# Average pooling on one core: a tapered end with the last rows in seven shrinking pieces, and smaller transfers around it

## Chip, cores, metric

One core of a Trainium2 chip. The metric is the device time of one execution in microseconds (us). "Span" is the profiled execution from its first to its last instruction; the device time of the same execution is 1.7 to 2.0 us longer. Verdicts use a threshold of 2%.

## The reference

```python
x = randn(32, 256, 4096).astype(float32)      # output_size = 256
for i in range(256):
    result[:, :, i] = np.mean(x[:, :, 16*i : 16*(i+1)], axis=-1)
```

That is 8192 rows of 4096 numbers, each reduced to 256 means of 16 neighbours: 134.22 MB are read, 8.39 MB are written, and each number takes part in one addition.

## The kernel before

A tile is 256 rows: 128 partitions with two adjacent rows each, so a partition's share is one run of 32 KB in memory. The load is issued from SyncE's queue, VectorE reduces, ScalarE scales, and the store is issued from ScalarE's queue. Four input buffers and eight output buffers let the stages overlap.

```python
    RPP = 2
    tile_rows = P * RPP
    assert N % tile_rows == 0
    ntiles = N // tile_rows

    x_t = x_flat.rearrange("(n p r) l -> n p (r l)", p=P, r=RPP)
    o_t = out_flat.rearrange("(n p r) g -> n p (r g)", p=P, r=RPP)

    inv_w = 1.0 / float(window)

    in_pool = ctx.enter_context(tc.tile_pool(name="in_pool", bufs=4))
    out_pool = ctx.enter_context(tc.tile_pool(name="out_pool", bufs=8))

    for i in range(ntiles):
        xt = in_pool.tile([P, RPP * L], x.dtype)
        nc.sync.dma_start(out=xt, in_=x_t[i])

        sums = out_pool.tile([P, RPP * O], mybir.dt.float32)
        nc.vector.reduce_sum(
            out=sums,
            in_=xt.rearrange("p (g w) -> p g w", w=window),
            axis=mybir.AxisListType.X,
        )
        means = out_pool.tile([P, RPP * O], mybir.dt.float32)
        nc.scalar.mul(out=means, in_=sums, mul=inv_w)
        nc.scalar.dma_start(out=o_t[i], in_=means)
```

## Time and profile before

| | value |
|---|---|
| device time, median of 4 | 346.53 us |
| span | 344.7 us |
| VectorE busy | 277.9 us, 81% |
| DMA, loads and stores, share of 16 engines | 90.4% + 6.3% |
| last load landed (start of the last reduction) | 332.46 us |

Lines of the page of the kernel before. The two rows of digits cut the span into 40 slices, each digit the busy tenths of a slice (9 is 90% or more). The two queue lines give packets, MB and the share of all 16 DMA engines' time. The group lines give operation, shapes and count, then busy us and mean ns of one, then the idle time ahead of them and what ended it.

```profile
span 344.7 us, 255 instructions
DVE  0488898888898888898888898887898888898885
DMA  8999999999999999999999999999999999999950
q1 hardware_dynamic: 4608, 134.22, 90.4%
q10 hardware_dynamic: 4608, 8.39, 6.3%
L50 DVE TENSOR_REDUCE sums<-xt 128x512 f32<-128x8192 f32 x32 | 277.9, 8686 | 63.2 <-DMA xt<-in_x_dram 63.2
```

DMA is full in every slice between the ends, while VectorE, though 81% busy, waits before each reduction, and always for a load. So the DMA engines bound the kernel, except after the last load. The timeline of its end (start, duration, what; in brackets the idle time before):

```profile
332.46 8.69 DVE L50 TENSOR_REDUCE sums<-xt 128x512 f32<-128x8192 f32 x1 [1.63 <-DMA xt<-in_x_dram]
341.18 0.63 ACT L56 ACTIVATE means<-sums 128x512 f32<-128x512 f32 x1 [9.68 <-DVE sums L50]
341.84 0.34 ACTq L57 DMA_DIRECT2D out_dram<-means  x1
```

These run in series after the last load, 12.2 us of the span, and the DMA engines are nearly idle meanwhile (a share of 0.07 from 333 to 334 us, 0.00 from there to 341, and 0.15 to 0.19 for the last store).

### The profile page before, as it was taken

What the parts mean: (1) busy time and instruction counts of PE and PEld (TensorE: products, weight loads), DVE (VectorE), ACT (ScalarE), POOL (GpSimd) and SP (SyncE); (2) the same over time, 40 slices, a digit from 0 to 9 for tenths busy, and PEclk for the clock granted to TensorE, in tenths of its full rate; (3) what the DMA queues carried; (4) which work ended last, traced back from release to release, by engine and by line L of the source; (5) the groups of instructions that cost most, each with busy time, mean ns of one, the idle gap of its engine ahead of it and who ended that gap; (6) DMA issues with size and microseconds to landing.
All of it is one profiled execution on the core that took longest, in us unless ns stands there. A gap on an engine that the chain in (4) does not pass through costs nothing.

```text
span 344.7 us, 255 instructions
## 1 busy us (share of the span) xinstructions
DVE 277.9 (81%) x32; ACT 21.4 (6%) x33; POOL 0.2 (0%) x4
## 2 busy tenths in 40 slices
DVE  0488898888898888898888898887898888898885
ACT  1000000000000000000000000000000000000000
POOL 0000000000000000000000000000000000000000
DMA  8999999999999999999999999999999999999950
GB/s 335 437 430 407 452 433 413 443 437 412 448 441 417 431 445 409 443 445 432 412 453 421 423 449 432 408 454 428 416 449 429 412 453 432 412 449 432 408 239 30
DMA packets 9217, 142.62 MB, mean 414 GB/s; under 512 B 1024, under 2 KB 1024, under 8 KB 5120
## 3 DMA queue, kind: packets, MB, share of 16 engines
q1 hardware_dynamic: 4608, 134.22, 90.4%
q10 hardware_dynamic: 4608, 8.39, 6.3%
q14 instruction: 1, 0.01, 0.0%
HBM read 134.22 MB, written 8.39 MB: 414 GB/s over the span
## 4 chain that ended last, share of the span: by engine, by line
DMA 78%; DVE 20%; SPq 0%; issue 0%; ACT 0%; DVEq 0%
DMA xt<-in_x_dram 78%; DVE sums L50 20%; SPq L47 0%; ACT means L56 0%; DVEq L50 0%
## 5 line engine op out<-in xcount | busy, mean ns | idle before, releaser
L50 DVE TENSOR_REDUCE sums<-xt 128x512 f32<-128x8192 f32 x32 | 277.9, 8686 | 63.2 <-DMA xt<-in_x_dram 63.2
L56 ACT ACTIVATE means<-sums 128x512 f32<-128x512 f32 x32 | 20.1, 629 | 319.7 <-DVE sums L50 319.7
L56 ACT ACT_TABLE_LOAD x1 | 1.3, 1283 | 0.7 <-PEq L74 0.7
L74 POOL MEMSET const-uint8-127<- 128x1 uint8 x1 | 0.1, 103 | 0.0
L74 POOL MEMSET const-bfloat16-1.0<- 128x1 bf16 x1 | 0.1, 102 | 0.0
L74 POOL MEMSET const-float32-1.0<- 128x1 f32 x1 | 0.1, 100 | 0.0
L74 POOL MEMSET const-float32-0.0<- 128x1 f32 x1 | 0.1, 99 | 0.2 <-issue 0.2
## 6 DMA issues: line engine op xcount, KB each, us to landing
xt<-in_x_dram SPq DMA_DIRECT2D x32, 4096.0 KB, 32.5
out_dram<-means ACTq DMA_DIRECT2D x32, 256.0 KB, 15.0
```

The lines of the kernel that those rows point to most:

```text
L50: nc.vector.reduce_sum(out=sums, in_=xt.rearrange("p (g w) -> p g w", w=window), axis=mybir.AxisListType.X,)
L56: nc.scalar.mul(out=means, in_=sums, mul=inv_w)
L74: nc = _bacc.Bacc("TRN2", target_bir_lowering=False, num_devices=1)
```

## The change

Its intent is to make that end short. The last group of 128 rows is loaded and reduced in seven pieces of 928 down to 224 columns, so that little is left to reduce when the last one lands. Before it come 15 half-size groups (one row per partition) and three groups in two or three pieces. The scaling is in place, three large buffers replace four, and the first tile is half-size. Below, "the split" is the cutting of the last group into seven pieces, and "the taper" the shrinking groups before it. The core of the diff (`...` marks what is left out; comments in it are shortened or added):

```diff
-    RPP = 2
-    tile_rows = P * RPP
 ...
-    ntiles = N // tile_rows
+    TAIL_SPLITS = [[L]] * 12 + [
+        [L],
+        [L],
+        [L],
+        [2560, 1536],
+        [2304, 1792],
+        [1664, 1408, 1024],
+        [928, 800, 704, 608, 496, 336, 224],
+    ]
+    n_tail = len(TAIL_SPLITS)
+    n_main = (n_groups - 1 - n_tail) // RPP          # 22 large tiles
 ...
+    NIN = 3                                          # large buffers
+    NTFRESH = 5                                      # half-size buffers
 ...  (first group: 128 rows on its own, then n_main large tiles as before, scaled in place)
+    for j in range(n_tail):
+        splits = TAIL_SPLITS[j]
+        buf = tail_in[j]      # halves of the large buffers, the last five fresh
+        ssum = tail_sums[j][:, :]
+        last = j == n_tail - 1
+        c0 = 0
+        for k, cc in enumerate(splits):
+            c1 = c0 + cc
+            nc.sync.dma_start(out=buf[:, c0:c1], in_=x_flat[r0 : r0 + P, c0:c1])
+            nc.vector.reduce_sum(out=ssum[:, c0 // window : c1 // window], ...)
+            if last and k == len(splits) - 4:        # scale and store the first 190 means
+                ...
+            c0 = c1
+        # scale and store the rest of the group (the last 66 means of the last group)
```

More of the change, by code (lines that the diff above doesn't have):

```diff
@@ L30 @@
     N = x_flat.shape[0]
-    RPP = 2
-    tile_rows = P * RPP
-    assert N % tile_rows == 0
-    ntiles = N // tile_rows
-    x_t = x_flat.rearrange("(n p r) l -> n p (r l)", p=P, r=RPP)
-    o_t = out_flat.rearrange("(n p r) g -> n p (r g)", p=P, r=RPP)
-    inv_w = 1.0 / float(window)
-    in_pool = ctx.enter_context(tc.tile_pool(name="in_pool", bufs=4))
-    out_pool = ctx.enter_context(tc.tile_pool(name="out_pool", bufs=8))
-    for i in range(ntiles):
-        xt = in_pool.tile([P, RPP * L], x.dtype)
-        nc.sync.dma_start(out=xt, in_=x_t[i])
-        sums = out_pool.tile([P, RPP * O], mybir.dt.float32)
+    inv_w = 1.0 / float(window)
@@ new lines @@
+    fp32 = mybir.dt.float32
+    if N % P != 0 or L % window != 0:
+        ntiles = (N + P - 1) // P
+        xb = nc.alloc_sbuf_tensor("xb", [P, L], x.dtype)
+        sb = nc.alloc_sbuf_tensor("sb", [P, O], fp32)
+        for i in range(ntiles):
+            r0 = i * P
+            r1 = min(N, r0 + P)
+            rr = r1 - r0
+            nc.sync.dma_start(out=xb[0:rr], in_=x_flat[r0:r1])
+            nc.vector.reduce_sum(
+                out=sb[0:rr],
+                in_=xb[0:rr].rearrange("p (g w) -> p g w", w=window),
+                axis=mybir.AxisListType.X,
+            )
+            nc.scalar.mul(out=sb[0:rr], in_=sb[0:rr], mul=inv_w)
+            nc.scalar.dma_start(out=out_flat[r0:r1], in_=sb[0:rr])
+        return
@@ new lines @@
+    n_groups = N // P
+    RPP = 2
+    first_rows = 16
+    TAIL_SPLITS = [[L]] * 12 + [
[8 more added lines that the diff above has]
+    n_tail = len(TAIL_SPLITS)
+    for s in TAIL_SPLITS:
+        assert sum(s) == L
+    n_main = (n_groups - 1 - n_tail) // RPP
+    main_rows = n_main * RPP * P
+    assert n_main > 0
+    assert P + main_rows + n_tail * P == N, (P, main_rows, n_tail * P, N)
@@ new lines @@
+    r_main0 = P
+    x_main = x_flat[r_main0 : r_main0 + main_rows].rearrange(
+        "(n p r) l -> n p (r l)", p=P, r=RPP
+    )
+    o_main = out_flat[r_main0 : r_main0 + main_rows].rearrange(
+        "(n p r) g -> n p (r g)", p=P, r=RPP
+    )
+    r_tail0 = r_main0 + main_rows
+    NIN = 3
+    in_bufs = [
+        nc.alloc_sbuf_tensor(f"xin{i}", [P, RPP * L], x.dtype) for i in range(NIN)
+    ]
+    NTFRESH = 5
+    tail_bufs = [
+        nc.alloc_sbuf_tensor(f"xtail{i}", [P, L], x.dtype) for i in range(NTFRESH)
+    ]
@@ new lines @@
+    g0_buf = tail_bufs[0]
+    NSUM = 4
+    sum_bufs = [
+        nc.alloc_sbuf_tensor(f"sums{i}", [P, RPP * O], fp32) for i in range(NSUM)
+    ]
+    g0_sum = nc.alloc_sbuf_tensor("sumg0", [P, O], fp32)
+    tail_sums = [
+        nc.alloc_sbuf_tensor(f"sumt{i}", [P, O], fp32) for i in range(n_tail)
+    ]
+    nc.sync.dma_start(out=g0_buf[:, :], in_=x_flat[0:P, :])
+    nc.vector.reduce_sum(
+        out=g0_sum[:, :],
+        in_=g0_buf[:, :].rearrange("p (g w) -> p g w", w=window),
+        axis=mybir.AxisListType.X,
+    )
@@ L50 @@
+    nc.scalar.mul(out=g0_sum[:, :], in_=g0_sum[:, :], mul=inv_w)
+    nc.scalar.dma_start(out=out_flat[0:P, :], in_=g0_sum[:, :])
+    for i in range(n_main):
+        xt = in_bufs[i % NIN][:, :]
+        nc.sync.dma_start(out=xt, in_=x_main[i])
+        st = sum_bufs[i % NSUM][:, :]
         nc.vector.reduce_sum(
-            out=sums,
+            out=st,
             in_=xt.rearrange("p (g w) -> p g w", w=window),
@@ L54 @@
         )
-        means = out_pool.tile([P, RPP * O], mybir.dt.float32)
-        nc.scalar.mul(out=means, in_=sums, mul=inv_w)
-        nc.scalar.dma_start(out=o_t[i], in_=means)
+        nc.scalar.mul(out=st, in_=st, mul=inv_w)
+        nc.scalar.dma_start(out=o_main[i], in_=st)
+    reuse_order = [(n_main - 3 + k) % NIN for k in range(NIN)]
+    tail_in = []
+    for j in range(n_tail):
+        if j < n_tail - NTFRESH:
+            h = (j % 2) * L
+            tail_in.append(in_bufs[reuse_order[j // 2 % NIN]][:, h : h + L])
+        else:
+            tail_in.append(tail_bufs[j - (n_tail - NTFRESH)][:, 0:L])
+    for j in range(n_tail):
+        r0 = r_tail0 + j * P
+        splits = TAIL_SPLITS[j]
[6 more added lines that the diff above has]
+            nc.sync.dma_start(out=buf[:, c0:c1], in_=x_flat[r0 : r0 + P, c0:c1])
+            nc.vector.reduce_sum(
+                out=ssum[:, c0 // window : c1 // window],
+                in_=buf[:, c0:c1].rearrange("p (g w) -> p g w", w=window),
+                axis=mybir.AxisListType.X,
+            )
+            if last and k == len(splits) - 4:
+                g1 = c1 // window
+                nc.scalar.mul(out=ssum[:, 0:g1], in_=ssum[:, 0:g1], mul=inv_w)
+                nc.scalar.dma_start(
+                    out=out_flat[r0 : r0 + P, 0:g1], in_=ssum[:, 0:g1]
+                )
+            c0 = c1
+        if last:
+            g0c = (L - sum(splits[-3:])) // window
+            nc.scalar.mul(out=ssum[:, g0c:O], in_=ssum[:, g0c:O], mul=inv_w)
+            nc.scalar.dma_start(
+                out=out_flat[r0 : r0 + P, g0c:O], in_=ssum[:, g0c:O]
+            )
+        else:
+            nc.scalar.mul(out=ssum, in_=ssum, mul=inv_w)
+            nc.scalar.dma_start(out=out_flat[r0 : r0 + P, :], in_=ssum)
 _INS = ['x', 'output_size']
```

## The prediction

> **What bounds the kernel now.** The 16 DMA engines. The page's slices show DMA at 9 (90% or more) from slice 2 to slice 38, at about 430 GB/s, while VectorE is 81% busy (277.9 us) and every one of its idle gaps (63.2 us) ends on a load. The timeline shows a reduction every 10.32 us: 8.69 us of work and 1.64 us of waiting. So in steady state only DMA work counts. The exposed parts are the ends: data starts to flow at about 2 us, and after the last load lands (332.4 us) the timeline runs in series: last reduction 332.46 to 341.15 (8.69), scaling 0.63, store and end 2.9, to 344.7. This 12.3 us tail is all that a better schedule can win; the measured time is 1.85 us over the span.
>
> **What the change does.**
> 1. Tail: the last row group is loaded and reduced in 7 shrinking pieces, so the last reduction is 224 elements, not 8192. This is the gain.
> 2. Everything else makes more, smaller transfers: 52 loads instead of 32, 43 stores instead of 32; half-size tiles for 15 of the last groups and the first one. In-place scaling, three large buffers rather than four and the early small first tile touch nothing that bounds: a released buffer still has over 11 us of queued loads before it.
>
> **Costs.** From the page's DMA queue table I work out 1217 ns per 32 KB load packet and 85 ns per 2 KB store packet (share x span x 16 / packets that carry data). A line through both gives about 8.7 ns fixed per packet. [...] Per engine the loads grow from 256 to 416 data packets (+1.4 us) and stores from 256 to 344 (+0.8 us), semaphore packets add 0.3: +2.5 us in all, estimated, on engines that are saturated, so all on the critical path. The last load then lands at about 335.0, not 332.4.
>
> The VectorE tail: [...] A piece's load takes about 1.18 ns per element plus 0.08 us[...]. Then scaling of 66 columns 0.26, store and end 2.6.
>
> End of span: 335.0 + 2.0 + 0.3 + 2.6 = 339.9; plus 1.85 gives 341.7 us, 1.4% faster. Of 8.3 us of reduction taken out of the tail, 2.5 go to packets and 2.0 to the backlog. Range 339.3 to 343.6. Chances: faster by over 2% (under 339.6) 0.15, within 2% 0.83, slower 0.02.
>
> **What the profile would show.** Load packets 16 KB at about 611 ns and data packets per queue as counted; DMA still at 9 up to about 335; last reduction ending 1 to 2.7 us after the last landing, with the last pieces back to back; then under 3.2 us to the end; steady state 10.3 us per large tile.
>
> **What would make it wrong.** The fixed packet cost hidden by overlap (2 us faster); piece loads held back because DMA semaphores are shared by few loads and stores, or bubbles between small loads (1 to 3 us slower); a smaller fixed cost per reduction (1 us faster); reductions and loads of one buffer serialised by the dependency tracking (several us slower).

The sum came to 339.9 us of span and 341.7 us of time. The derivation of its term 2.0, the time from the last landing to VectorE's end (1.0 to 2.7), followed the pieces of the last three groups with a formula for the time of a reduction by its size, and the trace of the kernel before has one size alone (8192 elements, 8686 ns). So the 2.0 stands as estimate, not as something shown. The 8.7 ns come from the page's queue table. The trace of the changed kernel shows the time of a piece's load (its packets take 3.08 us per engine for 2560 elements and 1.01 for 800; the prediction's figures give 3.10 and 1.02) and the scaling of 66 columns (0.26 us); the store and end of 2.6 is an estimate from the 2.9 of the kernel before.

## The result

The changed kernel takes 340.39 us (340.28 to 340.55, 8 runs) against 346.53 us (346.40 to 346.64, 12 runs). The ratio is 0.9824, 95% interval 0.9814 to 0.9833: 1.8% faster, within 2%. (A ratio is the mean time of one kernel's runs over that of the other's of the same rounds, so not quite the ratio of the medians.)

The same lines of the page after, with the groups that take the place of L50:

```profile
span 338.8 us, 325 instructions
DVE  0588887988888988889888889887999988988996
DMA  8999999999999999999999999999999999999995
q1 hardware_dynamic: 7488, 134.22, 92.5%
q10 hardware_dynamic: 6192, 8.39, 6.7%
L114 DVE TENSOR_REDUCE sums<-xin 128x512 f32<-128x8192 f32 x22 | 191.1, 8686 | 39.6 <-DMA xin<-in_x_dram 39.6
L141 DVE TENSOR_REDUCE sumt<-xin 128x256 f32<-128x4096 f32 x14 | 61.6, 4416 | 7.6 <-DMA xin<-in_x_dram 7.6
L141 DVE TENSOR_REDUCE sumt<-xtail 128x256 f32<-128x4096 f32 (+14 forms) x15 | 22.6, 1568 | 0.9 <-DMA xtail<-in_x_dram 0.8
```

The empty last DMA slices are gone, and over the last groups VectorE waits only 0.9 us before 15 reductions. There are more packets for the same bytes. The end in the view of the chain that ended last (start, duration, what each next step waited for):

```profile
326.93 5.37 DMA out_dram<-sumt
332.30 0.02 issue
332.32 0.33 SPq L140
332.64 0.04 issue
332.69 2.96 DMA xtail<-in_x_dram
335.65 0.02 issue
335.67 0.40 DVE sumt L141
336.07 0.02 issue
336.09 0.26 ACT sumt L155
```

The last piece landed at 335.65, its reduction took 0.40 us, and 2.69 us after that the span ended. So the stretch after the last load shrank from 12.2 to 3.1 us, while the last load landed 3.2 us later (335.65 against 332.46); the difference is the 5.9 us by which the span is shorter. One step surprises: the loads of the last two pieces (SPq L140) were issued only when an earlier store had landed (DMA out_dram<-sumt, 5.37 us). The waits in the trace's semaphore records say why. All 95 DMAs of this trace, loads and stores alike, take turns on eight semaphores, and one that takes a semaphore waits here until the DMA before it on that semaphore has landed. The 336-column load got the semaphore of the store of the third-last group: that store landed at 332.30, the load was issued at 332.32, and the 224-column load stood behind it in the queue (332.69).

The sum of the prediction against the trace:

| term | predicted | measured |
|---|---|---|
| last load lands | 335.0 | 335.65 |
| VectorE ends after it | 2.0 | 0.42 |
| scaling, store, end | 2.9 | 2.69 |
| span | 339.9 | 338.76 |
| median device time minus this span | 1.85 | 1.63 |

### The profile page after: what moved, and what is told of

It is laid out like the page before. It is cut to its first block, busy times and chain, and to the rows that moved or that the text cites. A ratio compares the mean times of both kernels' runs of the same rounds, so it can differ in the third digit from the quotient of the medians.

```text
span 338.8 us, 325 instructions
## 1 busy us (share of the span) xinstructions
DVE 279.6 (83%) x52; ACT 23.7 (7%) x44; POOL 0.2 (0%) x4
## 4 chain that ended last, share of the span: by engine, by line
DMA 76%; DVE 22%; SPq 0%; issue 0%; ACT 0%; DVEq 0%
DMA xin<-in_x_dram 68%; DVE sums L114 18%; DMA xtail<-in_x_dram 7%; DVE sumt L141 4%; DMA out_dram<-sumt 2%; SPq L112 0%; ACT sumt L160 0%; SPq L140 0%; SPq L101 0%; ACT sumt L155 0%; DVEq L114 0%
## 5 line engine op out<-in xcount | busy, mean ns | idle before, releaser
L114 DVE TENSOR_REDUCE sums<-xin 128x512 f32<-128x8192 f32 x22 | 191.1, 8686 | 39.6 <-DMA xin<-in_x_dram 39.6
L141 DVE TENSOR_REDUCE sumt<-xin 128x256 f32<-128x4096 f32 x14 | 61.6, 4416 | 7.6 <-DMA xin<-in_x_dram 7.6
L119 ACT ACTIVATE sums<-sums 128x512 f32<-128x512 f32 x22 | 13.8, 629 | 217.0 <-DVE sums L114 217.0
L141 DVE TENSOR_REDUCE sumt<-xtail 128x256 f32<-128x4096 f32 (+14 forms) x15 | 22.6, 1568 | 0.9 <-DMA xtail<-in_x_dram 0.8
L160 ACT ACTIVATE sumt<-sumt 128x256 f32<-128x256 f32 x18 | 7.5, 416 | 79.9 <-DVE sumt L141 79.9
L102 DVE TENSOR_REDUCE sumg<-xtail 128x256 f32<-128x4096 f32 x1 | 4.4, 4420 | 8.3 <-DMA xtail<-in_x_dram 8.3
## 6 DMA issues: line engine op xcount, KB each, us to landing
xin<-in_x_dram SPq DMA_DIRECT2D x22, 4096.0 KB, 22.2
```

Of the source, the lines that this page charges most:

```text
L102: nc.vector.reduce_sum(out=g0_sum[:, :], in_=g0_buf[:, :].rearrange("p (g w) -> p g w", w=window), axis=mybir.AxisListType.X,)
L114: nc.vector.reduce_sum(out=st, in_=xt.rearrange("p (g w) -> p g w", w=window), axis=mybir.AxisListType.X,)
L119: nc.scalar.mul(out=st, in_=st, mul=inv_w)
L141: nc.vector.reduce_sum(out=ssum[:, c0 // window : c1 // window], in_=buf[:, c0:c1].rearrange("p (g w) -> p g w", w=window), axis=mybir.Axi ...
L160: nc.scalar.mul(out=ssum, in_=ssum, mul=inv_w)
```

## The experiments

Two theories of why 12 us of tail became only 6 us of gain. A, the prediction's: each packet has a fixed cost on saturated DMA engines, and a backlog on VectorE eats a part. B, the rivals: packets are free, and the gain went to held-back loads, to too few buffers, or to groups that do no good.

### Shorter runs in the kernel before

```diff
-    x_t = x_flat.rearrange("(n p r) l -> n p (r l)", p=P, r=RPP)
-    o_t = out_flat.rearrange("(n p r) g -> n p (r g)", p=P, r=RPP)
+    x_t = x_flat.rearrange("(n r p) l -> n p r l", p=P, r=RPP)
+    o_t = out_flat.rearrange("(n r p) g -> n p r g", p=P, r=RPP)
 ...  (the two DMAs view their tiles to match)
```

> The kernel before, with the two rows of a partition taken 128 rows apart instead of adjacent. Same DMA count, same bytes, same buffers, same reductions; only each contiguous run halves, 16 KB loads and 1 KB stores. Theory A (a fixed cost of about 8.7 ns per data packet on saturated DMA engines): per engine 256 more load packets and 256 more store packets, 512 x 8.7 ns = 4.5 us, so about 351.0 us (350.2 to 351.8). Theory B (the packet cost is hidden by overlap, and the change lost its gain to VectorE or to waits of the loads): unchanged, 346.5 within 0.5.

Measured: 348.88 us against 346.50, ratio 1.0069 (1.0054 to 1.0084). Both numbers missed. 512 more packets per engine cost 2.4 us, 4.6 ns each and not 8.7. In the packet records the durations still are 611 ns for 16 KB and 46 ns for 1 KB, as the line through two points said, and they sum to 4.2 us more per engine than before. But durations of packets overlap (in the steady phase they add up to 1.01 of the engines' time, as shown below), so their sum is more than the time.

### The taper taken out

```diff
 (lines joined here)
-    TAIL_SPLITS = [[L]] * 12 + [ [L], [L], [L], [2560, 1536], [2304, 1792], [1664, 1408, 1024],
-        [928, 800, 704, 608, 496, 336, 224] ]
+    TAIL_SPLITS = [ [928, 800, 704, 608, 496, 336, 224] ]
 ...
-    NTFRESH = 5
+    NTFRESH = 1
```

> The changed kernel without the tapering groups: large tiles up to the last group, and only that one in the seven pieces. Theory A (VectorE works off its last large tile only 11 to 16% faster than data arrives, so a backlog needs several small groups to vanish): the seven pieces land about 333, but VectorE starts them only after the last 8.7 us reduction and ends near 340.5, span 343, time 344.9 (344 to 346.2). Theory B (the small last piece alone wins the tail): about 338 to 339.5, faster than the changed kernel since it has fewer packets.

Measured: 345.42 us, ratio 0.997: theory A, 0.5 us above its number. The timeline of the end:

```profile
327.71 8.69 DVE L108 TENSOR_REDUCE sums<-xin 128x512 f32<-128x8192 f32 x1 [1.68 <-DMA xin<-in_x_dram]
328.24 0.88 SPq L134 DMA_DIRECT2D xtail<-in_x_dram  x2
336.31 4.76 DVE L135 TENSOR_REDUCE sumt<-xtail 128x58 f32<-128x928 f32 x7
```

The seven pieces wait behind the last large reduction and run back to back, with no gap, until 341.07; the last of their loads had landed at 333.8. Splitting the last group without the groups that grow smaller towards it wins 1.1 us of the 6.1.

### The last group whole, the taper kept

```diff
-        [928, 800, 704, 608, 496, 336, 224],
+        [L],
 (the early store of the last group's first means is dropped with it)
```

> The changed kernel with its last group of 4096 elements loaded and reduced whole, its taper kept. Theory A: the last load lands about 0.5 us sooner (48 packets fewer), then a full reduction of 4.42 us, scaling 0.42 and the store: about 343.9 us (343.2 to 344.6), 3.5 us slower than the changed kernel. Theory B (the last split is worth little, since packets and held-back issues take back what it gains): within 1 us of the changed kernel's 340.4.

Measured: 344.02 us, ratio 0.9928 (0.9911 to 0.9944): theory A to 0.1 us. The end of its timeline:

```profile
334.84 4.42 DVE L141 TENSOR_REDUCE sumt<-xtail 128x256 f32<-128x4096 f32 x1 [3.68 <-DMA xtail<-in_x_dram]
339.30 0.42 ACT L155 ACTIVATE sumt<-sumt 128x256 f32<-128x256 f32 x1 [7.69 <-DVE sumt L141]
```

So each alone gives much less than both: the taper alone wins 2.5 us, the split alone 1.1, together 6.1.

### Three buffers

```diff
-    in_pool = ctx.enter_context(tc.tile_pool(name="in_pool", bufs=4))
+    in_pool = ctx.enter_context(tc.tile_pool(name="in_pool", bufs=3))
```

> The kernel before with three input buffers instead of four. Theory A (a freed buffer still has over 11 us of queued loads before it, so three are as good as four): 346.5 within 0.3. Theory B (fewer loads in flight starve the DMA engines, and part of the change's cost is this): over 347.5, with gaps in the DMA slices.

Measured: 346.58 us, ratio 1.0003 (0.9983 to 1.0023). In the kernel before, three input buffers take the same time as four. (In the changed kernel, with three, a large load lands 22.2 us after its issue, 10.3 of which are one tile's data, so about 11.9 us of other loads stand before it.)

### A shorter taper

```diff
-    TAIL_SPLITS = [[L]] * 12 + [
+    TAIL_SPLITS = [[L]] * 2 + [
```

> The changed kernel with 10 of its 15 whole half-size groups turned back into five large tiles. Theory A (packet cost, and five half-size groups are enough to work off VectorE's backlog): 40 load packets and 40 store packets fewer per engine, 0.7 us, 339.7 us (339.4 to 340.0). Theory B (packets free, or the backlog needs the long taper): 340.4 or slower.

Measured: 340.74 us (340.59 to 340.95), ratio 0.9832 (0.9818 to 0.9845): not faster, and not to be told from the changed kernel (0.9824). In its trace the last reduction ends at 335.6, 0.5 us sooner than in the changed kernel, and the last store lands at 337.43, 0.45 us sooner, but the span goes on 1.5 us after that instead of 0.9. Why this last stretch grew is open. That five whole half-size groups do as well as fifteen is shown.

### One store less near the end

```diff
+        # Groups n_tail-3 and n_tail-2 as one pair of rows per partition.
+        pair = j - (n_tail - 3) if n_tail - 3 <= j < n_tail - 1 else None
 ...
-            nc.scalar.dma_start(out=out_flat[r0 : r0 + P, :], in_=ssum)
+            if pair is None:
+                nc.scalar.dma_start(out=out_flat[r0 : r0 + P, :], in_=ssum)
+            elif pair == 1:          # both groups in one store
+                ...
```

> The changed kernel with the stores of its third- and second-last groups merged into one (rows paired per partition), so the loads of the last two pieces no longer share a DMA semaphore with a store that lands late. Theory A (VectorE's chain of pieces and the held-back last load end together, so taking the wait away moves the time little): 340.3, 0 to 0.3 us faster. Theory B (the held-back load bounds the end): 0.6 to 1.0 us faster, 339.6.

Measured: 340.51 us, ratio 0.9826 (0.9813 to 0.9840); the changed kernel, run again later, gave 340.53 and 0.9826. The chain that ended last has no store and no late issue in it any more:

```profile
318.63 9.94 DMA xtail<-in_x_dram
328.57 0.02 issue
328.59 2.75 DVE sump L151 x2
331.34 3.98 DVE sumt L151 x5
335.32 0.41 DVEq L208
335.73 0.30 DVE sumt L151
```

The late issue of the last loads is gone and the time is the same within the interval, so in the changed kernel it did not set the end by more than the noise. Theory A gave the reason, and the traces bear it out. The semaphore records have the last load (224 columns) landed at 334.96, 0.7 us sooner than in the changed kernel (335.65), but VectorE was not waiting for it. The reductions of all seven pieces run without a gap; here are the last three, of which the very last began at 335.65:

```profile
334.66 1.36 DVE L151 TENSOR_REDUCE sumt<-xtail 128x31 f32<-128x496 f32 x3
```

VectorE ended at 336.02, 1.06 us after that landing; in the changed kernel it ended at 336.06. There it waited 0.2 us in all for the last two pieces, but it had come to the last group 0.26 us sooner than here. When the changed kernel was run again, its last load landed at 335.51 and the last reduction began at 335.67. So in the changed kernel both ends, of the loads and of VectorE's chain, come within 0.2 us of each other. One load is still held in this version (608 columns, issued at 328.91 when a store had landed), but it landed at 333.61, before VectorE came to it at 333.97.

Each load lands in 16 parts (16 updates of its semaphore in the records). The slowest part of the last load came 0.9 us after the middle ones here (334.96 against 334.06), 0.6 us in the changed kernel (335.65 against 335.03) and 0.5 us in the kernel before (332.37 against 331.87). What makes one part late is open.

### Blocks of eight rows with large stores

```diff
-    RPP = 2
+    R = 8  # rows of one partition in one block: one store of R means
-    x_t = x_flat.rearrange("(n p r) l -> n p (r l)", p=P, r=RPP)
+    x_t = x_flat.rearrange("(n p r) l -> n p (r l)", p=P, r=R)
+    # Loads of a block, in elements of its partitions' rows.
+    plain = [2 * L] * (R // 2)
+    last = [L, L, L, L, 2560, 1536, 2304, 1792, 1664, 1408, 1024]
+    last += [928, 800, 704, 608, 496, 336, 224]
 ...  (means are scaled and stored per block; in the last block at 6 rows, and before the last 3 pieces)
```

> A version meant to beat both: eight adjacent rows per partition in a block, 32 KB load packets until the last block, one store of 8 KB packets per block, four half-size groups and the split groups in the last block. Theory A: per engine about 260 store packets and 40 load packets fewer than the changed kernel, 2.6 us, and the last semaphore waits gone: about 337.2 us (336.5 to 338.2). Theory B (packets hidden): 340.0 or more; a store of 1 MB at once or the larger row pitch could also cost something.

Measured: 340.27 us (339.96 to 340.41), ratio 0.9816 (0.9803 to 0.9830): theory A's 337.2 missed, and theory B's "340.0 or more" held. The next views compare the steady phases. A view of stretches has the stretch and its length, then busy us and count of VectorE, ScalarE and GpSimd, then clock, DMA share (above 1, as 1.01 here, where the durations of packets overlap) and GB/s. First the kernel before, over the large tiles (20 to 225 us):

```profile
20.00:225.00 205.00, 172.99 (x21) 12.58 (x20) 0.00 (x0) 1.00 1.01 431
```

The version with shorter runs:

```profile
20.00:225.00 205.00, 171.55 (x21) 12.58 (x20) 0.00 (x0) 1.00 1.01 429
```

The version with large stores:

```profile
20.00:225.00 205.00, 174.32 (x21) 9.55 (x5) 0.00 (x0) 1.00 1.00 431
```

And the changed kernel over its large tiles, then over its half-size groups (240 to 310 us):

```profile
20.00:225.00 205.00, 172.59 (x21) 12.58 (x20) 0.00 (x0) 1.00 1.01 432
240.00:310.00 70.00, 62.44 (x15) 6.04 (x14) 0.00 (x0) 1.00 1.01 427
```

With 8 KB store packets in place of 2 KB ones a fourth as many store packets are written, and the rate did not rise at all (431 GB/s both times). With half as long runs of loads and stores it fell (429). That points at the loads.

Another thing cost this version its gain. In its trace (of the fastest of its four runs) the last load landed at 333.9 and the last reduction ended at 334.45, 1.6 us sooner than in the changed kernel, but its last two stores landed 1.3 us after their last packet; in the changed kernel that took 0.4 us. Its last stores go to rows 8 KB apart, those of the changed kernel to rows 1 KB apart.

### Loads in short runs, then stores in short runs

Each is the kernel before with a padded tile on one side, so that one DMA breaks into four runs per partition with no other change.

```diff
-        xt = in_pool.tile([P, RPP * L], x.dtype)
-        nc.sync.dma_start(out=xt, in_=x_t[i])
+        xt = in_pool.tile([P, 4, RPP * L // 4 + 16], x.dtype)
+        xv = xt[:, :, 0 : RPP * L // 4]
+        nc.sync.dma_start(out=xv, in_=x_t[i].rearrange("p (c l) -> p c l", c=4))
 ...  (the reduction reads the same four runs)
```

> The kernel before, with each load cut into four runs of 8 KB per partition by a padded input tile; addresses in HBM, DMA count and stores unchanged. Per engine 1024 load packets instead of 256. After the first run of short runs (2.4 us for 256 load and 256 store packets) two theories are left. Theory C (a load packet costs its 8.7 ns in full, a store packet's is hidden behind loads on the other queue): 768 x 8.7 ns = 6.7 us, 353.2 us (352.6 to 353.8). Theory D (each packet of either kind costs about half, 4.6 ns): 3.6 us, 350.1 us.

Measured: 352.15 us, ratio 1.0163 (1.0148 to 1.0178): 5.7 us for 768 load packets, 7.4 ns each, between the theories and nearer to C. The reductions still took 8686 ns each, so VectorE has no part in it. The same stretch:

```profile
20.00:225.00 205.00, 169.62 (x21) 12.59 (x20) 0.00 (x0) 1.00 1.01 425
```

Put into the run with shorter runs, 256 load packets at 7.4 ns make 1.9 of its 2.4 us, which leaves 0.5 us for 256 store packets, about 1.9 ns each (an estimate from these two runs; their intervals are 0.5 us wide to each side, so it can't be told from zero). By these two runs a load packet pays most of the 8.7 ns (7.4 ns), and most of a store packet's is hidden (1.9 ns are seen, by the estimate).

```diff
-        means = out_pool.tile([P, RPP * O], mybir.dt.float32)
-        nc.scalar.dma_start(out=o_t[i], in_=means)
+        means = out_pool.tile([P, 4, RPP * O // 4 + 16], mybir.dt.float32)
+        mv = means[:, :, 0 : RPP * O // 4]
 ...  (the scaling writes into mv)
+        nc.scalar.dma_start(out=o_t[i].rearrange("p (c g) -> p c g", c=4), in_=mv)
```

> The kernel before, with each store cut into four runs of 512 B per partition by a padded tile of means; loads, DMA count and addresses in HBM unchanged. Per engine 1024 store packets instead of 256. Theory C (store packets are hidden): within 0.7 us of 346.5. Theory D (half cost for each): 768 x 4.6 ns = 3.6 us, 350.1 us. Full cost: 353.2 us. A cost only for store packets above one per load packet would also show as 4 to 7 us.

Measured: 365.70 us, ratio 1.0551. No theory expected this much, and the run doesn't measure the cost of a packet. Its waits (engine and line, for what: us in total, times, longest):

```profile
ACT means L57 <- issue: 239.6, 7, 67.5
DVE sums L50 <- ACT means L57: 53.3, 3, 24.7
```

and two lines of its timeline:

```profile
135.15 29.19 ACTq L60 DMA_DIRECT2D out_dram<-means  x1
198.44 8.69 DVE L50 TENSOR_REDUCE sums<-xt 128x512 f32<-128x8192 f32 x1 [24.71 <-ACT means L57]
```

Issuing one store took ScalarE 29 us instead of 0.34; ScalarE stood still, then VectorE, and then the loads. While both queues were full (240 to 310 us) the packet records have 0.81 load packets and 0.88 store packets per us and engine: nearly one for one, though a load packet was 32 KB and a store packet 512 B. A tile has 8 load packets and here 32 store packets per engine, so at these rates the stores could not keep up with the loads. That this backlog is what blocked the issue is inferred. In the kernel before a tile has 8 of each (0.78 and 0.76 per us), and its stores keep up: those issued at 104 and at 301 us both landed 15.0 us later.

### Fewer packets with the rows of the changed kernel, and the changed kernel again

28 large tiles, then 8 groups of 128 rows in the pieces of the changed kernel's last 8, their stores merged:

```diff
 (parts, lines joined)
+    n_tail = 8  # groups of P rows at the end
 ...
+    splits = [[L]] * 4 + [ [2560, 1536], [2304, 1792], [1664, 1408, 1024],
+        [928, 800, 704, 608, 496, 336, 224] ]
+    stores = {1: 0, 4: 2, 6: 5}  # last group of a store: its first
 ...
+        if j in stores:
+            finish(o_j[:, stores[j] : j + 1, :], ts[:, stores[j] : j + 1, :])
```

> A version from what the runs showed: 28 large tiles, then 8 groups of 128 rows as the changed kernel has its last 8; 368 load packets per engine instead of 416; stores of the last groups merged to four, so that no late load shares a semaphore with a late store; the last rows laid out as in the changed kernel, not eight to a partition as in the version with big stores, whose last stores took 1.3 us instead of 0.4 to report their landing. Expected under theory C: last load lands near 334.0, VectorE ends near 334.7, span 337.4, 339.1 us (338.6 to 339.8), 1.2 us faster than the changed kernel on the same chip. Rival (the end of the changed kernel is bound by something else that the trace doesn't show): 340.0 or more.

> The changed kernel itself, unaltered, so that the versions can be compared on one chip: 340.4 within 0.3 under every theory.

Measured: 342.14 us, ratio 0.9872; the changed kernel in the same rounds 340.53 us, 0.9826. So it is 1.6 us slower than the changed kernel, for a reason of its own. Its chain:

```profile
322.41 8.50 DMA out_dram<-ts
330.90 0.02 issue
330.92 3.69 DMA xt<-in_x_dram
```

and its stretches around there:

```profile
330.00:331.00 1.00, 1.00 (x2) 0.63 (x1) 0.00 (x0) 1.00 0.76 298
331.00:332.00 1.00, 1.00 (x2) 0.00 (x0) 0.00 (x0) 1.00 0.16 31
332.00:333.00 1.00, 1.00 (x2) 0.00 (x0) 0.00 (x0) 1.00 0.83 141
```

A merged store of three groups landed 8.5 us after its issue; that its 24 packets per engine, served about one for one with load packets as in the run with stores in short runs, made it so late is inferred. The load of the 608-column piece shared its semaphore, was issued at 330.92, and the DMA engines ran dry, to a share of 0.16; VectorE then stood idle from 333.05 to about 334.6. This is the held-back load again, and by this trace it does set the end here. I had judged that this store would land in time, which was wrong.

### Large stores, with the last rows apart

Against the version with large stores, in part:

```diff
+    # The last block in three: 5, 2 and 1 adjacent rows per partition.
-    cuts = [6 * L, R * L - 496 - 336 - 224, R * L]
+    cuts = [5 * L, 7 * L, R * L - 496 - 336 - 224, R * L]
```

> The version with big stores (340.27 us), with only the last 8 groups laid out anew: five adjacent rows per partition, then two, then one, each stored on its own, so the very last stores go to rows 1 KB apart instead of 8 KB apart. Same number of DMAs, and no late load shares a semaphore with a late store. In the version with big stores the last two stores landed 1.3 us after their last packet, in the changed kernel 0.4 us after. If the distance of the rows written is the cause: 0.4 us again, about 339.3 us (338.9 to 339.8), a good 1 us faster than the changed kernel. If it is not, the landing stays at 1.3 us and the time near 340.2.

Measured: 340.06 us, but from 339.43 to 340.77, ratio 0.9809 (0.9796 to 0.9823). The last two stores landed 0.3 and 0.6 us after their last packet, so the distance of the rows is the likely cause of the 1.3 us (the grouping of the rows changed with it). A held-back load stands in the chain again:

```profile
322.27 6.84 DMA out_dram<-sums
329.11 0.02 issue
329.12 0.33 SPq L77
```

But the DMA engines did not run dry after it (a share of 0.97 or more until 333 us), and VectorE waited 0.6 us in all for the last pieces. That the held-back load cost the 0.8 us between 339.3 and 340.06 is not shown.

This version is the fastest by its median, but its interval overlaps those of the changed kernel. None of the runs gave a version that is clearly faster.

## Why the prediction was right, and where it was not

The range held: 341.7 predicted, 340.39 measured, and a gain of 6.1 us instead of 4.8. Point by point:

- **The bound.** Right. Over the large tiles the rate is 431 GB/s before and 432 after; in the half-size groups it is 427. Three buffers are as good as four (346.58 against 346.50 us).
- **"Everything else makes more, smaller transfers."** This named the split as the gain and all else as cost. The step failed: the taper is as necessary as the split. Without the taper the kernel takes 345.42 us. After a large tile VectorE is 8.7 us behind and gains little per tile, because data for a large tile take 10.32 us and its reduction 8.69. Without the taper it ended 7.3 us after the last load (341.07 against 333.8), with successively smaller reductions before the last group 0.42 us after it. The estimate of the backlog used the taper without saying so.
- **"+2.5 us in all" for packets.** Mis-sized. The packet durations sum to 2.5 us more per engine (333.4 to 335.9 in the records; 0.28 of it are packets of 4 bytes, 9 ns each), exactly as predicted, but they overlap. At 7.4 ns per load packet and 1.9 ns per store packet, the change's 160 and 88 packets make 1.35 us (an estimate). (With the rounded 1217 and 85 of the prediction the line's fixed part is 9.5 ns; the mean records, 1215.9 and 84.1, give 8.7.)
- **"The last load then lands at about 335.0."** It landed at 335.65, later in spite of cheaper packets, so something was left out. One part is bytes: the kernel before writes its last two stores almost wholly after its last load, 0.68 us of DMA time each (8 packets of 85 ns per engine); the changed kernel leaves only its last 1 KB per partition, so about 1 us of stores moved ahead of the last load (an estimate). Another is the held-back issue: in the version with one store less the last load landed at 334.96. The slowest of the load's 16 parts, 0.6 us after the middle ones, explains little, since in the kernel before it was 0.5. How these parts add up is not shown. That 335.0 came as near as it did is partly luck: packets were put too high, and moved stores and held-back issues left out.
- **The backlog of "2.0 us".** Mis-sized: 0.42. It was reckoned from the durations of single reductions. The trace of the changed kernel has 8686 ns for 8192 elements, 4416 for 4096 and 385 for 224; a line through the first two has 1.04 ns per element and 146 ns fixed, and gives 380 for the third (an estimate). But back to back the reductions overlap: in the timeline of the changed kernel

```profile
333.79 1.35 DVE L141 TENSOR_REDUCE sumt<-xtail 128x38 f32<-128x608 f32 x2
334.48 1.58 DVE L141 TENSOR_REDUCE sumt<-xtail 128x31 f32<-128x496 f32 x3
```

  the 608-column reduction starts at 333.79 and the next at 334.48 (merged lines start with the first of their reductions): 0.69 us, where its own duration in the trace is 0.775. So a reduction in a chain costs about 0.09 us less than its duration, over some ten pieces about 1 us (an estimate). The prediction had "a smaller fixed cost per reduction (1 us faster)" among its risks. The remaining 0.6 us is as much as the last load itself came later, which gave VectorE time to catch up. The version with one store less bears this out: with the last load at 334.96 VectorE ended 1.06 us after it, at 336.02, as against 336.06 in the changed kernel.
- **Held-back loads.** Named as a risk of 1 to 3 us. They happened, but in the changed kernel cost nothing measurable: without them the last load landed 0.7 us sooner, and VectorE's chain of pieces ended no sooner. In the version with merged stores, by its trace, the same mechanism set the end, and that kernel was 1.6 us slower than the changed one.

The central value was 1.3 us too high because the errors partly cancelled: landing +0.65, backlog -1.6, the rest -0.4. The first two belong together: a later landing leaves less backlog.

## What to carry to other kernels

When DMA bounds a kernel, try a taper and a split of its end together, since here each alone gave much less (2.5 and 1.1 us, together 6.1): work out for each size how far the consuming engine is behind when the data land. Count a fixed cost per contiguous run for loads (7.4 ns here); measure it by the time of a whole run, not by adding packet durations, which overlapped here (they added up to 4.2 us more where the time grew by 2.4). And look at which DMAs share a semaphore: here late loads waited for stores that landed 5.4 to 8.5 us after their issue.
